# Seven-product stage: key rope, query norm and query rope one gate pair later, bank copies first; first products of the last projection ahead of the last head

## The chip, the cores and the metric

One core of a Trainium2 chip runs the program. Its engines work side by side, each through its own queue in order: TensorE (PE) multiplies matrices into the eight banks of PSUM, VectorE (DVE) and ScalarE (ACT) work element by element, GpSimd (POOL) and SyncE (SP) issue transfers. The metric is the device time of one execution in microseconds, as the median of several runs.

## What is computed

A trunk of two layers over a sequence of 1024 positions with 1024 features, all in float32. The first layer is a gated linear recurrence. The second is attention with eight heads whose keys and values come from a compressed vector; a gate multiplies its result ahead of the output projection. The part that the change touches is this one:

```python
def mla_shared_kv(x_stream, norm_kv, w_dkv, kv_norm, w_uk, w_uv, cos, sin):
    h = rms_norm(x_stream, norm_kv)
    ckr = h @ w_dkv
    c_kv = rms_norm(ckr[..., :KV_RANK], kv_norm)
    k_rope = apply_rope(ckr[..., KV_RANK:], cos[None], sin[None])
    k_nope = jnp.einsum("bsc,chd->bshd", c_kv, w_uk)
    v = jnp.einsum("bsc,chd->bshd", c_kv, w_uv)
    return k_nope, k_rope, v

def mla_layer(x, norm_g, w_in, q_norm, w_uq, w_out, k_nope, k_rope, v, cos, sin):
    h = rms_norm(x, norm_g)
    u = h @ w_in
    c_q = rms_norm(u[..., :Q_RANK], q_norm)
    gate = u[..., Q_RANK:]
    q = jnp.einsum("bsc,chd->bshd", c_q, w_uq)
    q_nope = q[..., :QK_NOPE]
    q_rope = apply_rope(q[..., QK_NOPE:], cos[None, :, None], sin[None, :, None])
    o = causal_block_attention(q_nope, q_rope, k_nope, k_rope, v)
    y = o.reshape(bsz, seq, N_HEADS * V_DIM) * jax.nn.silu(gate)
    return y @ w_out
```

A last norm over the features closes the trunk.

## The kernel before

Every float32 operand of a product is split into a high and a low part, and three matmuls (L114, L115, L116: high by high, low by high, high by low) stand for one. ACT rounds the high part (L82), DVE subtracts it for the low part (L83). A tile is 128 partitions by 512 elements; `hs(h)` is one of the two halves of the sequence, `page()` a tile of 128 by 1024 from a ring of 36, `tk()` a half tile from a ring of 8.

The linear recurrence fills the first 360 us or so. Then comes the stage that the names call `pair(m, ...)`. It makes two output blocks of 128 features for both halves of the sequence, four blocks of products, with seven products in place of eight, in the manner of Strassen. A product (`fmul`) is 12 matmuls, a pair 84. PE makes them into four PSUM banks a, c, b, d in the order a, c, b, a again, d, c again, d again. Between them banks are copied by ACT (`copy`, L611): a into b, once a's first product is there, then c into a spare tile `cc`, b into d, and b into a spare tile `v2`; the next product is added onto the copy. DVE takes the results out (L631, L162). The weights of a product are tiles `wa`, scaled by ACT (L507), summed by DVE (L519) and split (`wh`, `wl`).

Six such pairs follow one another, with other work between them: pair 0 gives the compressed key and value (`kvt`), pair 2 the key's rope input `krt` and the first third of the query, pair 4 the other two thirds (`qt`). Then come four gate pairs, `pair(6 + j)` with j = 0, 2, 4 and 6, numbered 6, 8, 10 and 12, each giving the gates of two heads, which ACT passes through Silu (L786) and POOL's queue stores in `gd`. The last of them takes its banks (`pm`) from the attention's pool, on the same PSUM. Work of the query and key lies beside the gate pairs:
- the key rope (L748 to L751): per half three DVE operations and a `spill`, which splits the result and stores it;
- the query's norm: its sums of squares on PE in the middle of pair 6 (L685), DVE's root (L150, L151), then multiplications of `qt` (L698, the function `multiplies` in `normed`) and a split of the six halves into `cq`;
- the query rope, `qrope(g)`: 72 matmuls in eight banks, and for each of four bank pairs two sums of two multiplications on DVE (L764 to L766), each split by ACT and DVE and stored by POOL's queue.

Program order gives the order of the work, with one correction: instructions are placed by a scheduler, in whose eyes those inside `tc.high_priority(offset=n)` stand n earlier. The order on each engine is then fixed; an engine waits for the instruction at the head of its queue. The copies have offset 120 (`WPC`) in before.

The attention runs over 64 items, a head and a block of 128 queries: scores (L867 to L871), a softmax (reduce L874, exponent L877, normalising L879), transposes (L887) and, for four blocks together, the product with the values, `pv` (L902 to L904), whose result DVE multiplies by the gate (L906) and splits. `pv` runs `PVD` items after its blocks, three after in head 6's second half. The last projection runs after the last head, but 36 of its matmuls (`dpart`, 12 parts of three) are placed inside the last head by the table `D_AT`. `wout` loads a block of its weight and makes the low part (L933); `yload` brings back the results of earlier heads.

Of the kernel before, what the change touches and what calls it, by code (L numbers as in the profile page):

```python
# [12 lines left out]
ALU = mybir.AluOpType  # L13
# [8 lines left out]
NH = 8  # L22
# [4 lines left out]
NPAGES = 36  # L27
NSPILL = 6
WPRI = 100
WOUT_AT = (-1, 1, 2)  # L30
YL_AT = (0, 0, 0, 0, 1, 2)
DSTART = 0
DPART = tuple((dt, k, k + 1) for dt in range(2) for k in range(6))
DEPQ = "gpsimd"
LOOK = 2
KQ_AT = (1, 0, 1, 0, 2, 0, 0, 0)
V0_AT = (1, 1, 2, 0)
V_AT = (0, 0, 0, 0, 0, 0, 1, 1)
D_AT = (0, 4, 1, 1, 1, 0, 3, 2)
PVD = 1  # L40
VQB = 4
HW = 512
# [7 lines left out]
GADD = ()  # L50
NWA = 7
WPC = 120


NA, CW, CB, BR, BI, LAM, NKV, KVN, NB, QN, FN, NVEC = 0, 8, 48, 58, 68, 78, 88, 96, 98, 106, 109, 117
# [2 lines left out]
def trunk(tc, xT, wina, vecs, wgate, wouta, winc, wuk, wuv, wuq, wuqr, woutb, rope, outT):  # L58
# [64 lines left out]
    def hs(h):  # L123
        return slice(h * HW, (h + 1) * HW)
# [478 lines left out]
    def pair(m, dst, w, banks, raw=(False, False), mid=None):  # L603

        a, c, b, d = banks
        cc = tcp.tile([P, HW], F32, tag="cc", bufs=2, name=nm("cc"))
        v2 = tcp.tile([P, HW], F32, tag="v2", name=nm("v2"))

        def copy(dst_, src, scale=1.0):
            with tc.high_priority(offset=WPC):  # L610
                A.activation(out=dst_, in_=src, func=AF.Copy, scale=scale)  # L611

        fmul(a, w[0], 0, True)
        copy(b, a, -1.0)
        fmul(c, w[1], 1, True)
        copy(cc, c)
        fmul(b, w[2], 2, False)
        fmul(a, w[3], 4, False)
        copy(d, b)
        copy(v2, b)  # L620
        fmul(d, w[4], 3, False)
        rest = mid() if mid else None

        def put(i, h, src):
            if raw[i]:
                A.activation(out=dst[i][h], in_=src, func=AF.Copy)
            else:
                byr(dst[i][h], src, r1[:, hs(h)])

        def put2(i, h, x, y):  # L630
            V.tensor_tensor(out=dst[i][h], in0=x, in1=y, op=ALU.subtract)  # L631
            if not raw[i]:
                byr(dst[i][h], dst[i][h], r1[:, hs(h)])

        put2(1, 1, d, cc)
        put(0, 0, a)
        fmul(c, w[5], 6, False)
        put2(0, 1, c, v2)
        fmul(d, w[6], 5, False)
        put(1, 0, d)  # L640
        if rest:
            rest()

    def wa():
        return tcp.tile([P, HW], F32, tag="wa", bufs=NWA, name=nm("wa"))
# [1 line left out]
    def four():  # L647
        return [pst() for _ in range(4)]

    def halves(t):  # L650
        return [t[:, hs(0)], t[:, hs(1)]]
# [36 lines left out]
    def normed(ts, acc, ps_, gcol, fac):  # L688
        n = len(ts)
        gs = con.tile([P, n], F32, name=nm("gs"))  # L690
        V.tensor_scalar(out=gs, in0=vec[:, gcol:gcol + n], scalar1=-0.5 * fac, scalar2=None, op0=ALU.mult)
        total(acc, ps_, P * n)

        def multiplies():
            for h in range(2):
                for j in range(n):
                    t = ts[j][:, hs(h)]
                    V.scalar_tensor_tensor(out=t, in0=t, scalar=gs[:, j:j + 1], in1=acc[h], op0=ALU.mult, op1=ALU.mult)  # L698

        return multiplies  # L700
# [8 lines left out]
    kvps = presum(kvacc)  # L709
    krt = page(F32)  # L710
    qt = [page(F32) for _ in range(3)]
    pair(2, [halves(krt), halves(qt[0])], wpair(2, wa), four(), (False, True), lambda: normed(kvt, kvacc, kvps, KVN, 1.0))
    square(qt, qacc, 0)


# [27 lines left out]
    for j in range(1, 3):  # L743
        square(qt, qacc, j)
    qps = presum(qacc)
    for h in range(2):
        x, y = krt[:, hs(h)], krs[:, hs(h)]
        V.tensor_tensor(out=x, in0=x, in1=cs[:, hs(h)], op=ALU.mult)  # L748
        V.scalar_tensor_tensor(out=y, in0=y, scalar=sgn, in1=sn[:, hs(h)], op0=ALU.mult, op1=ALU.mult)
        V.tensor_tensor(out=x, in0=x, in1=y, op=ALU.add)  # L750
        spill(4, h, x)  # L751


    qsd = dp.tile([4, 2 * P, S], F32, name="qsd")
# [18 lines left out]
    for j in range(0, NH, 2):  # L773
        gts = [[tk(), tk()] for _ in range(2)]
        w = wpair(6 + j, wa)
        if j < NH - 2:
            banks = four()
        else:

            pp.close()  # L780
            pss = es.enter_context(tc.tile_pool(name="pss", bufs=2, space=PSUM, reuse_waits="tile"))
            banks = [pss.tile([P, HW], F32, tag="pm", bufs=4, name=nm("pm")) for _ in range(4)]
        pair(6 + j, gts, w, banks, mid=None if j else lambda: normed(qt, qacc, qps, QN, SCALE))
        for i in range(2):
            for h in range(2):
                A.activation(out=gts[i][h], in_=gts[i][h], func=AF.Silu)  # L786
                DQ.dma_start(out=gd[j + i, :, hs(h)], in_=gts[i][h])
        if j == 0:
            cq = []
            for t in qt:  # L790
                cq.append((page(), page()))
                for h in range(2):
                    hl(t[:, hs(h)], cq[-1][0][:, hs(h)], cq[-1][1][:, hs(h)])
            cs, sn = tables()
        elif j == 2:
            for g in range(2):
                qrope(g)

# [159 lines left out]
    for i, (hd, qb) in enumerate(items):  # L958
# [19 lines left out]
        g = qb // 4  # L978
        if qb % 4 == 0:
            pts[hd, g] = [tuple(tp.tile([P, 4, HW], F32R, tag=f"pt{i}", name=nm("pt")) for i in range(2)) for _ in range(g + 1)]  # L980

        if late and i - late[0][0] >= (PVD if (hd, qb) < (NH - 2, 4) or hd == NH - 1 else 3):
            pv(*late.pop(0)[1:])
        transposes(qb, pend.pop((hd, qb)), pts[hd, g])
        if qb % 4 == 3:
# [138 lines left out]
```

## Time and profile before

| what | us |
|---|---|
| median of 3 runs (873.95 to 874.32) | 874.07 |
| the profiled execution's own time | 874.96 |
| its span | 873.2 |
| PE busy | 856.7 |
| DVE busy | 659.2 |
| ACT busy | 517.1 |
| POOL busy | 73.6 |

The mean granted clock of PE is 0.995 of full speed. A row of the timeline reads: start, duration, engine, line, operation, output and inputs with their shapes, how many, and in brackets the idle time of the engine ahead of it and what ended it. A row of waits reads: who waited for whom, total in us, how often, the longest. A matmul of 512 columns is shown as 0.39 us long, but they overlap: one starts each 0.227 us. In the same way DVE's and ACT's rows overlap by some 0.1 us.

### The profile page before, as it was taken

What the parts mean: (1) busy time and instruction counts of PE and PEld (TensorE: products, weight loads), DVE (VectorE), ACT (ScalarE), POOL (GpSimd) and SP (SyncE); (2) the same over time, 40 slices, a digit from 0 to 9 for tenths busy, and PEclk for the clock granted to TensorE, in tenths of its full rate; (3) what the DMA queues carried; (4) which work ended last, traced back from release to release, by engine and by line L of the source; (5) the groups of instructions that cost most, each with busy time, mean ns of one, the idle gap of its engine ahead of it and who ended that gap; (6) DMA issues with size and microseconds to landing.
All of it is one profiled execution on the core that took longest, in us unless ns stands there. A gap on an engine that the chain in (4) does not pass through costs nothing.

```text
span 873.2 us, 12181 instructions
## 1 busy us (share of the span) xinstructions
PE 856.7 (98%) x4326; PEld 729.3 (84%) x4326; DVE 659.2 (75%) x1222; ACT 517.1 (59%) x956; POOL 73.6 (8%) x143
## 2 busy tenths in 40 slices
PE   8999999999999999999999999999999999999995
PEld 7788888888888888888778889888998998888995
DVE  6898788777877764769889957888797887775453
ACT  7457787777687543699885545555565554431222
POOL 1010110011000100001211320000000000010000
PEclk9999999999999999999999999999999999999998
DMA  8333333333213544133545674122231326666032
GB/s 292 96 97 97 97 96 98 109 101 93 79 37 91 169 156 152 49 108 114 184 143 176 215 242 132 52 88 91 70 112 67 116 63 259 217 210 207 27 125 67
DMA packets 51789, 109.00 MB, mean 125 GB/s; under 512 B 6544, under 2 KB 16656, under 8 KB 51728
## 3 DMA queue, kind: packets, MB, share of 16 engines
q1 hardware_dynamic: 35968, 67.19, 24.0%
q0 software_dynamic: 15216, 40.51, 14.1%
q8 instruction: 34, 0.56, 0.3%
q10 hardware_dynamic: 544, 0.52, 0.2%
q14 instruction: 27, 0.22, 0.1%
HBM read 81.46 MB, written 26.21 MB: 123 GB/s over the span
## 4 chain that ended last, share of the span: by engine, by line
PE 90%; ACT 3%; DVE 3%; DMA 1%; issue 1%; POOL 0%; DVEq 0%; SPq 0%; ACTq 0%; POOLq 0%
PE ps L114 17%; PE ps L115 17%; PE ps L116 17%; PE pm L116 6%; PE pm L115 6%; PE pm L114 6%; PE pm L887 3%; PE pm L903 2%; PE pm L904 2%; PE s L868 2%; PE pm L902 2%; PE s L870 2%; PE s L869 2%; PE s L871 2%; PE s L867 2%
## 5 line engine op out<-in xcount | busy, mean ns | idle before, releaser
L114 PE MATMUL ps<-pg,wh 128*128 128x512 f32 x672 | 263.1, 392 | 4.7 <-ACT ps L611 2.2
L115 PE MATMUL ps<-pg,wh 128*128 128x512 f32 x672 | 262.1, 390 | 0.0
L116 PE MATMUL ps<-pg,wl 128*128 128x512 f32 x672 | 262.1, 390 | 0.1
L114 PEld LDWEIGHTS ps<-pg,wh 128*128 128x128 f32 x672 | 126.5, 188 | 33.7 <-ACT ps L611 3.9
L116 PEld LDWEIGHTS ps<-pg,wl 128*128 128x128 f32 x672 | 126.4, 188 | 26.8 <-DVE wl L83 0.4
L115 PEld LDWEIGHTS ps<-pg,wh 128*128 128x128 f32 x672 | 126.5, 188 | 26.6 <-DVE pg L262 0.5
L82 ACT ACTIVATE pt<-pm 128x512 fp32r<-128x512 f32 (+2 forms) x96 | 44.3, 490 | 59.3 <-PE pm L887 54.5
L877 ACT ACTIVATE pg<-s,m 128x128 f32<-128x128 f32 (+3 forms) x64 | 47.5, 743 | 45.1 <-DVE m L874 40.3
L114 PE MATMUL pm<-pg,pg 128*128 128x256 f32 (+1 forms) x192 | 61.9, 322 | 0.0
L115 PE MATMUL pm<-pg,pg 128*128 128x256 f32 (+1 forms) x192 | 61.6, 321 | 0.0
L116 PE MATMUL pm<-pg,pg 128*128 128x256 f32 (+1 forms) x192 | 61.3, 319 | 0.0
L83 DVE TENSOR_TENSOR pt<-pm,pt 128x512 fp32r<-128x512 f32 (+2 forms) x96 | 50.5, 547 | 2.3 <-ACT pt L82 2.3
L874 DVE TENSOR_REDUCE m<-s 128x1 f32<-128x128 f32 (+3 forms) x64 | 48.1, 754 | 1.1
L82 ACT ACTIVATE wh<-wr 128x512 fp32r<-128x512 f32 (+2 forms) x57 | 30.9, 543 | 25.9 <-PE ps L115 15.2
L358 DVE SCALAR_TENSOR_TENSOR t<-xb,vec,t 128x512 f32<-128x512 f32 x60 | 44.8, 747 | 0.4
L83 DVE TENSOR_TENSOR wl<-wr,wh 128x512 fp32r<-128x512 f32 (+2 forms) x57 | 32.9, 579 | 16.0 <-ACT wh L82 15.8
L82 ACT ACTIVATE pg<-pg 128x512 fp32r<-128x512 f32 x42 | 26.1, 630 | 30.1 <-DVE pg L412 17.9
L887 PE MATMUL pm<-ident,pg 128*128 128x128 f32 x288 | 42.3, 274 | 0.7 <-DVE pg L906 0.7
L116 PE MATMUL pm<-pg,wl 128*128 128x512 f32 x108 | 42.3, 392 | 0.0
L115 PE MATMUL pm<-pg,wh 128*128 128x512 f32 x108 | 42.3, 392 | 0.0
L114 PE MATMUL pm<-pg,wh 128*128 128x512 f32 x108 | 42.1, 390 | 0.0
L114 PEld LDWEIGHTS pm<-pg,pg 128*128 128x128 f32 x192 | 36.6, 191 | 2.6 <-issue 0.2
(226 smaller groups left out, 1787.5 us busy)
## 6 DMA issues: line engine op xcount, KB each, us to landing
wr<-wina SPq DMA_DIRECT2D x40, 256.0 KB, 2.9
wh<-wina POOLq DMA_DIRECT2D x36, 256.0 KB, 2.9
wa<-winc SPq DMA_DIRECT2D x24, 256.0 KB, 3.1
ysd<-pg POOLq DMA_DIRECT2D x12, 512.0 KB, 3.2
pg<-ysd SPq DMA_DIRECT2D x12, 512.0 KB, 9.9
wr<-wouta SPq DMA_DIRECT2D x16, 256.0 KB, 2.7
t<-xT SPq DMA_DIRECT2D x16, 256.0 KB, 3.8
x1d<-t POOLq DMA_DIRECT2D x16, 256.0 KB, 2.5
```

What stands on the lines that cost most here:

```text
L82: A.activation(out=hi, in_=src, func=AF.Copy)
L83: V.tensor_tensor(out=lo, in0=src, in1=f(hi), op=ALU.subtract)
L114: T.matmul(out=ps, lhsT=w[0], rhs=r[0], start=first, stop=False, skip_group_check=more)
L115: T.matmul(out=ps, lhsT=w[0], rhs=r[1], start=False, stop=False, skip_group_check=more)
L116: T.matmul(out=ps, lhsT=w[1], rhs=r[0], start=False, stop=last, skip_group_check=more)
L358: V.scalar_tensor_tensor(out=xc, in0=xb[:, j:j + HW], scalar=cwv[j], in1=xc, op0=ALU.mult, op1=ALU.add)
L867: T.matmul(out=sc[:, c], lhsT=q[0][:, ql], rhs=k[0][:, c], start=True, stop=False)
L868: T.matmul(out=sc[:, c], lhsT=q[0][:, ql], rhs=k[1][:, c], start=False, stop=False)
L869: T.matmul(out=sc[:, c], lhsT=q[1][:, ql], rhs=k[0][:, c], start=False, stop=False)
L874: V.tensor_reduce(out=m, in_=sc, axis=AX.X, op=ALU.max, negate=True)
L877: A.activation(out=p_[:, 0:nk], in_=sc, func=AF.Exp, bias=m, accum_out=l)
L887: T.transpose(out=ps[:, (b - b0) * P:(b - b0 + 1) * P], in_=p_[:, b * P:(b + 1) * P], identity=ident)
```

## The change

- The copies' offset becomes 600 (`WPB`); that of the other work that uses `WPC` stays at 120.
- The key rope becomes a function and is issued after pair 6 in place of before it.
- `pair` hands back the function of the norm's multiplications in place of calling it. For the query it is called after pair 8 (before: at the end of pair 6), and the split into `cq` goes with it. For the compressed key and value it is called at once, as before.
- `qrope` is issued after pair 10 (before: after pair 8).
- In the last head, the first weight block of the last projection is loaded and split four items earlier, `yload` begins five items earlier, and the parts of three matmuls are spread by another table from one item earlier on.
- `pv` of head 6's second half runs one item after its blocks, in place of three.

```diff
--- before.py
+++ after.py
@@ -27,16 +27,16 @@
 NPAGES = 36
 NSPILL = 6
 WPRI = 100
-WOUT_AT = (-1, 1, 2)
-YL_AT = (0, 0, 0, 0, 1, 2)
-DSTART = 0
+WOUT_AT = (-5, 1, 2)
+YL_AT = (-5, -4, 0, 0, 1, 2)
+DSTART = -1
 DPART = tuple((dt, k, k + 1) for dt in range(2) for k in range(6))
 DEPQ = "gpsimd"
 LOOK = 2
 KQ_AT = (1, 0, 1, 0, 2, 0, 0, 0)
 V0_AT = (1, 1, 2, 0)
 V_AT = (0, 0, 0, 0, 0, 0, 1, 1)
-D_AT = (0, 4, 1, 1, 1, 0, 3, 2)
+D_AT = (2, 0, 3, 1, 1, 1, 0, 2, 2)
 PVD = 1
 VQB = 4
 HW = 512
@@ -50,6 +50,7 @@
 GADD = ()
 NWA = 7
 WPC = 120
+WPB = 600
 
 
 NA, CW, CB, BR, BI, LAM, NKV, KVN, NB, QN, FN, NVEC = 0, 8, 48, 58, 68, 78, 88, 96, 98, 106, 109, 117
@@ -607,7 +608,7 @@
         v2 = tcp.tile([P, HW], F32, tag="v2", name=nm("v2"))
 
         def copy(dst_, src, scale=1.0):
-            with tc.high_priority(offset=WPC):
+            with tc.high_priority(offset=WPB):
                 A.activation(out=dst_, in_=src, func=AF.Copy, scale=scale)
 
         fmul(a, w[0], 0, True)
@@ -638,8 +639,7 @@
         put2(0, 1, c, v2)
         fmul(d, w[6], 5, False)
         put(1, 0, d)
-        if rest:
-            rest()
+        return rest
 
     def wa():
         return tcp.tile([P, HW], F32, tag="wa", bufs=NWA, name=nm("wa"))
@@ -709,7 +709,7 @@
     kvps = presum(kvacc)
     krt = page(F32)
     qt = [page(F32) for _ in range(3)]
-    pair(2, [halves(krt), halves(qt[0])], wpair(2, wa), four(), (False, True), lambda: normed(kvt, kvacc, kvps, KVN, 1.0))
+    pair(2, [halves(krt), halves(qt[0])], wpair(2, wa), four(), (False, True), lambda: normed(kvt, kvacc, kvps, KVN, 1.0))()
     square(qt, qacc, 0)
 
 
@@ -743,12 +743,14 @@
     for j in range(1, 3):
         square(qt, qacc, j)
     qps = presum(qacc)
-    for h in range(2):
-        x, y = krt[:, hs(h)], krs[:, hs(h)]
-        V.tensor_tensor(out=x, in0=x, in1=cs[:, hs(h)], op=ALU.mult)
-        V.scalar_tensor_tensor(out=y, in0=y, scalar=sgn, in1=sn[:, hs(h)], op0=ALU.mult, op1=ALU.mult)
-        V.tensor_tensor(out=x, in0=x, in1=y, op=ALU.add)
-        spill(4, h, x)
+
+    def krope():
+        for h in range(2):
+            x, y = krt[:, hs(h)], krs[:, hs(h)]
+            V.tensor_tensor(out=x, in0=x, in1=cs[:, hs(h)], op=ALU.mult)
+            V.scalar_tensor_tensor(out=y, in0=y, scalar=sgn, in1=sn[:, hs(h)], op0=ALU.mult, op1=ALU.mult)
+            V.tensor_tensor(out=x, in0=x, in1=y, op=ALU.add)
+            spill(4, h, x)
 
 
     qsd = dp.tile([4, 2 * P, S], F32, name="qsd")
@@ -780,19 +782,23 @@
             pp.close()
             pss = es.enter_context(tc.tile_pool(name="pss", bufs=2, space=PSUM, reuse_waits="tile"))
             banks = [pss.tile([P, HW], F32, tag="pm", bufs=4, name=nm("pm")) for _ in range(4)]
-        pair(6 + j, gts, w, banks, mid=None if j else lambda: normed(qt, qacc, qps, QN, SCALE))
+        rest = pair(6 + j, gts, w, banks, mid=None if j else lambda: normed(qt, qacc, qps, QN, SCALE))
         for i in range(2):
             for h in range(2):
                 A.activation(out=gts[i][h], in_=gts[i][h], func=AF.Silu)
                 DQ.dma_start(out=gd[j + i, :, hs(h)], in_=gts[i][h])
         if j == 0:
+            krope()
+            qnorm = rest
+        elif j == 2:
+            qnorm()
             cq = []
             for t in qt:
                 cq.append((page(), page()))
                 for h in range(2):
                     hl(t[:, hs(h)], cq[-1][0][:, hs(h)], cq[-1][1][:, hs(h)])
             cs, sn = tables()
-        elif j == 2:
+        elif j == 4:
             for g in range(2):
                 qrope(g)
 
@@ -978,8 +984,7 @@
         g = qb // 4
         if qb % 4 == 0:
             pts[hd, g] = [tuple(tp.tile([P, 4, HW], F32R, tag=f"pt{i}", name=nm("pt")) for i in range(2)) for _ in range(g + 1)]
-
-        if late and i - late[0][0] >= (PVD if (hd, qb) < (NH - 2, 4) or hd == NH - 1 else 3):
+        if late and i - late[0][0] >= PVD:
             pv(*late.pop(0)[1:])
         transposes(qb, pend.pop((hd, qb)), pts[hd, g])
         if qb % 4 == 3:
```

In these rows of an engine's order stand line, operation, output, inputs and size; the numbers in the names tell tiles apart and differ between the kernels. First ACT, around the end of the query rope. Before, the pair behind the rope is pair 10: `tk` rows of L82 are splits of the rope, `wh` rows splits of weights, L611 the copy of bank a into b.

```order
L82 ACTIVATE tk_825_4267<-tk_824_4266 128x512
L82 ACTIVATE wh_862_4438<-ws_861_4436 128x512
L82 ACTIVATE tk_827_4276<-tk_826_4275 128x512
L82 ACTIVATE tk_831_4305<-tk_830_4304 128x512
L82 ACTIVATE wh_864_4443<-ws_861_4436 128x512
L507 ACTIVATE wa_895_4616<-wa_895_4616,vec_66 128x128 x4
L82 ACTIVATE tk_833_4314<-tk_832_4313 128x512
L82 ACTIVATE wh_867_4453<-wa_866_4447 128x512
L82 ACTIVATE wh_869_4458<-wa_856_4414 128x512
L611 ACTIVATE ps_877_4473<-ps_875_4471 128x512
L82 ACTIVATE tk_843_4355<-tk_842_4354 128x512
```

Now the pair behind the rope is pair 12, whose banks are named `pm`:

```order
L83 ACTIVATE wh_891_4607<-ws_890_4605 128x512
L83 ACTIVATE tk_856_4445<-tk_855_4444 128x512
L83 ACTIVATE tk_860_4474<-tk_859_4473 128x512
L83 ACTIVATE wh_893_4612<-ws_890_4605 128x512
L83 ACTIVATE tk_862_4483<-tk_861_4482 128x512
L83 ACTIVATE wh_896_4622<-wa_895_4616 128x512
L83 ACTIVATE tk_872_4524<-tk_871_4523 128x512
L83 ACTIVATE tk_874_4533<-tk_873_4532 128x512
L83 ACTIVATE tk_878_4562<-tk_877_4561 128x512
L83 ACTIVATE tk_880_4571<-tk_879_4570 128x512
L83 ACTIVATE wh_898_4627<-wa_885_4583 128x512
L612 ACTIVATE pm_906_4646<-pm_904_4644 128x512
```

Four splits of the rope stood ahead of the copy before, with a fifth behind it; now all eight do (the first is the row ahead of those shown), and the weight split `wh_898`.

On DVE, the end of the rope's work in the changed kernel (L766 and L767 are the multiplications, L768 the sums, the L84 rows with `tk` the low parts of the splits):

```order
L766 TENSOR_TENSOR tk_873_4532<-ps_869_4503,pg_815_4231 128x512
L767 TENSOR_TENSOR tk_874_4533<-ps_870_4504,pg_814_4230 128x512
L84 TENSOR_TENSOR tk_871_4523<-tk_871_4523,tk_872_4524 128x512
L768 TENSOR_TENSOR tk_873_4532<-tk_873_4532,tk_874_4533 128x512
L766 TENSOR_TENSOR tk_877_4561<-ps_875_4541,pg_814_4230 128x512
L767 TENSOR_TENSOR tk_878_4562<-ps_876_4542,pg_815_4231 128x512
L84 TENSOR_TENSOR tk_873_4532<-tk_873_4532,tk_874_4533 128x512
L768 TENSOR_TENSOR tk_877_4561<-tk_877_4561,tk_878_4562 128x512
L766 TENSOR_TENSOR tk_879_4570<-ps_875_4541,pg_815_4231 128x512
L767 TENSOR_TENSOR tk_880_4571<-ps_876_4542,pg_814_4230 128x512
L84 TENSOR_TENSOR tk_877_4561<-tk_877_4561,tk_878_4562 128x512
L768 TENSOR_TENSOR tk_879_4570<-tk_879_4570,tk_880_4571 128x512
```

Between the fourth sum and the eighth, which is the last row here, stand these rows and six more; of pair 12's weights only one split and one sum lie among them.

Second, ACT in the first gate pair, from the copy of a into b to the two copies of bank b. Before:

```order
L611 ACTIVATE ps_768_3911<-ps_766_3909 128x512
L82 ACTIVATE tk_737_3822<-tk_635_3280 128x512
L507 ACTIVATE wa_801_4102<-wa_801_4102,vec_66 128x128
L82 ACTIVATE tk_739_3826<-tk_636_3281 128x512
L82 ACTIVATE tk_741_3833<-pg_663_3430 128x512
L611 ACTIVATE cc_770_3913<-ps_767_3910 128x512
L82 ACTIVATE wh_762_3901<-wa_757_3885 128x512
L507 ACTIVATE wa_856_4414<-wa_856_4414,vec_66 128x128 x4
L82 ACTIVATE wh_764_3905<-wa_749_3864 128x512
L611 ACTIVATE ps_769_3912<-ps_768_3911 128x512
L611 ACTIVATE v2_771_3914<-ps_768_3911 128x512
```

And now:

```order
L612 ACTIVATE ps_766_3895<-ps_764_3893 128x512
L83 ACTIVATE tk_737_3822<-tk_635_3280 128x512
L508 ACTIVATE wa_793_4074<-wa_793_4074,vec_66 128x128
L83 ACTIVATE tk_739_3826<-tk_636_3281 128x512
L83 ACTIVATE wh_760_3885<-wa_755_3869 128x512
L612 ACTIVATE cc_768_3897<-ps_765_3894 128x512
L508 ACTIVATE wa_820_4238<-wa_820_4238,vec_66 128x128 x4
L83 ACTIVATE wh_762_3889<-wa_747_3848 128x512
L612 ACTIVATE ps_767_3896<-ps_766_3895 128x512
L612 ACTIVATE v2_769_3898<-ps_766_3895 128x512
```

The split of the key rope (`tk_741`) has left; the four scalings (L507) and the weight split stay ahead of the copies of bank b.

Third, DVE where head 6 ends. A block's normalising (L879) has the width of its keys, 896 for the block before the last, 1024 for the last; head 7's first block has 128. Before, from two rows behind the normalising of the block before the last:

```order
L83 TENSOR_TENSOR pg_1422_7088<-pm_1456_7268,pg_1421_7087 128x512
L83 TENSOR_TENSOR pt_1458_7278<-pm_1461_7281,pt_1457_7277 128x4x128
L872 TENSOR_TENSOR s_1463_7292<-s_1463_7292,mask_80 128x128
L874 TENSOR_REDUCE m_1464_7304<-s_1463_7292 128x1
L83 TENSOR_TENSOR pt_1458_7278<-pm_1467_7311,pt_1457_7277 128x4x128
L872 TENSOR_TENSOR s_1469_7323<-s_1469_7323,mask_80 128x128
L874 TENSOR_REDUCE m_1470_7330<-s_1469_7323 128x1
L878 RECIPROCAL l_1466_7307<-l_1466_7307 128x1
L879 TENSOR_SCALAR pg_1465_7306<-pg_1465_7306,l_1466_7307 128x1024
L878 RECIPROCAL l_1472_7333<-l_1472_7333 128x1
L879 TENSOR_SCALAR pg_1471_7332<-pg_1471_7332,l_1472_7333 128x128
L906 TENSOR_TENSOR pg_1414_7073<-pm_1473_7337,pg_1414_7073 128x512
```

And now, from the normalising (L885) of the third last block, 768 wide, on:

```order
L885 TENSOR_SCALAR pg_1448_7228<-pg_1448_7228,l_1449_7229 128x768
L880 TENSOR_REDUCE m_1458_7265<-s_1457_7253 128x1
L939 TENSOR_TENSOR pg_1454_7245<-wr_1455_7246,pg_1453_7244 128x512
L939 TENSOR_TENSOR pg_1454_7245<-wr_1456_7250,pg_1453_7244 128x512
L884 RECIPROCAL l_1460_7268<-l_1460_7268 128x1
L912 TENSOR_TENSOR pg_1414_7073<-pm_1467_7294,pg_1414_7073 128x512
L885 TENSOR_SCALAR pg_1459_7267<-pg_1459_7267,l_1460_7268 128x896
L84 TENSOR_TENSOR pg_1422_7088<-pm_1461_7272,pg_1421_7087 128x512
L84 TENSOR_TENSOR pg_1422_7088<-pm_1462_7281,pg_1421_7087 128x512
L84 TENSOR_TENSOR pg_1469_7309<-pg_1414_7073,pg_1468_7308 128x512
L84 TENSOR_TENSOR pt_1464_7291<-pm_1470_7312,pt_1463_7290 128x4x128
```

The two subtractions of the first weight block (L939) and the gate product of head 6's first half (L912, before L906) now stand ahead of the normalising of the block before the last, and so ahead of the last block's.

## The prediction

> **What bounds the kernel now.** The page comes first: its engine table, its chain, and the row of the costliest group.
>
> ```profile
> span 873.2 us, 12181 instructions
> ...
> PE 856.7 (98%) x4326; PEld 729.3 (84%) x4326; DVE 659.2 (75%) x1222; ACT 517.1 (59%) x956; POOL 73.6 (8%) x143
> ...
> PE 90%; ACT 3%; DVE 3%; DMA 1%; issue 1%; POOL 0%; DVEq 0%; SPq 0%; ACTq 0%; POOLq 0%
> ...
> L114 PE MATMUL ps<-pg,wh 128*128 128x512 f32 x672 | 263.1, 392 | 4.7 <-ACT ps L611 2.2
> ```
>
> TensorE (PE) is busy for 98% of the span and makes up 90% of the chain. The diff neither adds nor removes a matmul, so only PE's idle time can change, and the clock at which PE runs. Next come the waits of PE between 20 and 860 us, and, of the timeline, the matmul behind each of the larger ones:
>
> ```profile
> PE ps L114 <- ACT ps L611: 2.2, 3, 1.3
> PE ps L114 <- DVE tk L631: 1.1, 1, 1.1
> PE pm L887 <- DVE pg L906: 0.7, 1, 0.7
> PE pm L903 <- DVE pt L83: 0.3, 1, 0.3
> ```
>
> ```profile
> 430.75 0.50 PE L114 MATMUL ps<-pg,wh 128*128 128x512 f32 x1 [1.31 <-ACT ps L611]
> ...
> 437.09 0.50 PE L114 MATMUL ps<-pg,wh 128*128 128x512 f32 x1 [0.60 <-ACT ps L611]
> ...
> 447.67 0.50 PE L114 MATMUL ps<-pg,wh 128*128 128x512 f32 x1 [1.15 <-DVE tk L631]
> ```
>
> That is all there is to win: 1.31 + 0.60 + 1.15 = 3.1 us in the first gate pair, 0.3 in the pair before it, and 0.7 + 0.3 = 1.0 in the last head. A pause longer than about 4 us does not exist inside the kernel, so a new one would count in full.
>
> **Bank copies and the first gate pair: 0.** The higher priority should let the copies (L611) pass other work on ACT. For each of the three waits I ask what ends last, by ACT's and DVE's timelines:
>
> ```profile
> 421.98 0.60 ACT L626 ACTIVATE pg<-ps 128x512 f32<-128x512 f32 x1 [2.01 <-DMA kvd<-pg]
> ...
> 430.12 0.58 ACT L611 ACTIVATE ps<-ps 128x512 f32<-128x512 f32 x1
> ...
> 434.75 1.28 ACT L507 ACTIVATE wa<-wa,vec 128x128 f32<-128x128 f32 x4 [0.23 <-DMA wa<-winc]
> 435.94 0.61 ACT L82 ACTIVATE wh<-wa 128x512 fp32r<-128x512 f32 x1
> 436.46 0.57 ACT L611 ACTIVATE ps<-ps 128x512 f32<-128x512 f32 x1
> ```
>
> ```profile
> 441.99 0.69 DVE L83 TENSOR_TENSOR wl<-ws,wh 128x512 fp32r<-128x512 f32 x1 [1.29 <-ACT wh L82]
> ...
> 446.93 0.68 DVE L631 TENSOR_TENSOR tk<-ps,cc 128x512 f32<-128x512 f32 x1
> ```
>
> The first wait goes back to a spill that ACT waits for at 421.98; behind that, the changed order has the same ACT rows up to the copy at 430.12. The second copy still stands behind four scalings of a weight tile (L507), which start when its DMA lands, at 434.75. What leaves the queue ahead of it is a split of the key rope, which had room in front of that DMA. The third is DVE's queue of ten operations between 441.99 and 447.5; they are all still there. So I take no gain here. The ends are 0 and -3.4 (all four waits gone). The 0.3 of the pair before may go, but the matmul at 430.75 then waits that much longer, since its copy is tied to the spill.
>
> **Query rope behind the third gate pair: +7.2.** This is the large term. ACT works its queue in order: the copy of bank a into bank b, for which PE waits two products into a pair, cannot start before the rows ahead of it. Before, four of the query rope's eight splits stood ahead of it in the pair behind the rope; now, by the order shown with the change, all eight do, and PE's rope is followed at once by the last gate pair. How late the splits are is read from before, where the rope also runs:
>
> ```profile
> 466.86 0.39 PE L114 MATMUL ps<-pg,wh 128*128 128x512 f32 x1
> ...
> 483.18 0.39 PE L114 MATMUL ps<-pg,wh 128*128 128x512 f32 x1
> ```
>
> ```profile
> 482.45 0.68 DVE L766 TENSOR_TENSOR tk<-tk,tk 128x512 f32<-128x512 f32 x1
> ...
> 496.13 0.69 DVE L766 TENSOR_TENSOR tk<-tk,tk 128x512 f32<-128x512 f32 x1
> ```
>
> ```profile
> 483.21 0.63 ACT L82 ACTIVATE tk<-tk 128x512 fp32r<-128x512 f32 x1 [0.18 <-ACT wa L507]
> 483.75 0.62 ACT L82 ACTIVATE wh<-wa 128x512 fp32r<-128x512 f32 x1
> ...
> 486.47 0.58 ACT L611 ACTIVATE ps<-ps 128x512 f32<-128x512 f32 x1
> ```
>
> Let T be the rope's first matmul, 466.86 in before. The rope has 72 matmuls and ends at 483.18, T + 16.3, so one takes 0.227 us. The next pair's two first products are 24 matmuls, 5.4 us. PE is therefore due at the third product at T + 21.8. In before the copy ran at 486.47, T + 19.6, and was in time by 2 us; the matmul follows a copy by 430.75 - 430.12 = 0.63.
>
> Now the changed kernel. DVE makes eight sums (L766), each behind two multiplications, and each sum releases one split on ACT. The fourth sum stood at 482.45, T + 15.6, in before; the work up to it is the same in both. From there to the eighth, DVE's changed queue has 18 instructions: 8 multiplications, 4 sums, 4 low-part subtractions, one weight split and one weight sum. DVE had no pause there in before: 22 steps from 482.45 to 496.13 make 0.62 each, so 18 take 11.2. The eighth sum starts at T + 26.8 and ends at T + 27.5. Behind it on ACT stand the eighth split, one weight split and the copy. A split occupies the queue for 0.54 (483.21 to 483.75), so the copy starts at T + 28.6 and PE at T + 29.2. That is 7.4 late, or 7.0 if a step is 0.60. I take 7.2. Ends: 5.4 if DVE needs 0.5 for a step, 8.5 if the last weight split's DMA or bank adds a microsecond. The wait is not hidden: the last pair's two first products are all that PE has, and behind the copy wait the remaining 60 matmuls and the attention. That the third pair now has no rope ahead of it frees nothing, since in before its copy was in time.
>
> **The clock behind that pause: +1.7.** No pause of this length is in the trace, so I bound the price. The nearest rows are those of the start, a matmul behind a pause and the windows that follow (their columns are length, busy time of PE, PEld, DVE, ACT and POOL, granted clock, DMA share), and, on the other side, the first gate pair's window:
>
> ```profile
> 6.11 0.51 PE L114 MATMUL ps<-pg,wh 128*128 128x512 f32 x1 [1.38 <-ACT wh L82]
> ```
>
> ```profile
> 7.00:9.00 2.00, 2.00 (x4) 1.11 (x5) 1.23 (x2) 0.97 (x2) 0.00 (x0) 0.60 1.02 396
> 9.00:10.80 1.80, 1.80 (x5) 1.43 (x5) 0.70 (x2) 1.67 (x2) 0.00 (x0) 0.50 0.96 373
> ...
> 430.00:449.00 19.00, 16.50 (x70) 12.97 (x71) 15.61 (x26) 14.80 (x35) 2.22 (x4) 1.00 0.37 122
> ```
>
> In the start the clock stood at half for about 2 x 0.8 + 1.8 = 3.4 us; work at half clock loses half of that, 1.7. Pauses of 1.3 us in mid-kernel cost no clock. A pause of 7 us is nearer to the sparse start than to these, so I take one such stretch, 1.7, with ends at 0 and 3.4 (two stretches).
>
> [...]
>
> **Key rope and query norm one pair later: 0.** They are the same DVE and ACT instructions, now beside the gate pairs 8 and 10 in place of 6 and 8. DVE's share there is the cover:
>
> ```profile
> 449.00:468.00 19.00, 19.00 (x86) 15.71 (x85) 16.83 (x28) 17.59 (x39) 3.79 (x7) 1.00 0.66 209
> 483.00:503.00 20.00, 20.00 (x90) 16.58 (x89) 19.65 (x33) 10.86 (x20) 7.58 (x14) 1.00 0.63 219
> ```
>
> The pair at 449 to 468 leaves DVE 2.2 us and ACT 1.4 us of room. The normalising of the query, 6 products and 12 splits, moves out of it, and the key rope's 6 products and its splits and four spills come in. The rope's own window leaves DVE 0.35 us; its work is what leaves. The spills go through the POOL queue, which is busy for 3.79 of 19 us. If the room were missed in either pair, the price is a copy late by one or two ACT rows, at most 1 us together.
>
> **First products of the last projection ahead of the last head: +0.4.** The waits there, and the rows they come from:
>
> ```profile
> 740.42 0.45 PE L902 MATMUL pm<-pt,pg 128*128 128x512 f32 x1
> ...
> 742.34 0.62 PE L887 MATMUL pm<-ident,pg 128*128 128x128 f32 x4
> ...
> 744.30 1.42 PE L887 MATMUL pm<-ident,pg 128*128 128x128 f32 x11 [0.74 <-DVE pg L906]
> ...
> 747.28 0.50 PE L903 MATMUL pm<-pt,pg 128*128 128x512 f32 x1 [0.33 <-DVE pt L83]
> ```
>
> ```profile
> 743.56 0.68 DVE L906 TENSOR_TENSOR pg<-pm,pg 128x512 f32<-128x512 f32 x1
> ...
> 750.73 1.28 DVE L933 TENSOR_TENSOR pg<-wr,pg 128x512 fp32r<-128x512 f32 x2
> ```
>
> These waits hang on the softmax chain of head 6's last query block. The p times v product of that head's first half (12 matmuls, 740.42 to 742.34, 1.9 us) now runs ahead of that block's scores, its gate product (L906, 0.6 from start to start) and the first weight's two subtractions (1.2) stand ahead of its normalising on DVE. The chain is later by 1.9 + 0.6 + 1.2 = 3.7. PE has 1.9 of that as moved work and 6 of the 36 pulled-forward matmuls of the last projection, 1.4, as cover: 3.3. So 0.4 more of waiting; ends -1.0 (both waits covered) and +1.3 (the subtractions in full).
>
> **Sum.** Against the profiled execution's own time, 874.96 with a span of 873.2, the change is +7.2 + 1.7 + 0.4 = +9.3. The median of the runs shown is 874.07, 0.9 lower, and the timed runs are what is forecast: 874.07 + 9.3 = **883.4**.
>
> **The rivals.**
> (a) The wait comes but the clock holds: 874.07 + 7.2 + 0.4 = 881.7. For it speaks that no mid-kernel pause lowered the clock, against it that none was over 1.5 us. 0.22.
> (b) The wait comes, and the first gate pair's copies do pass: 883.4 - 3.4 = 880.0. Against it stand the DMA at 434.75 and the spill at 421.98, which no priority moves. 0.08.
> (c) Two stretches at half clock in place of one, since the pause drops the clock late or the clock rises late: 883.4 + 1.7 = 885.1. For it: the pause is five times as long as the one at 6.11. Against it: the start, which had one stretch. [...] 0.12.
> (d) The other side: DVE keeps pace with PE's rope, the last pair's copy is in time, and the four early waits and the last head's go: 874.07 - 3.4 - 1.0 = 869.7. It decides at the copy's start: T + 21.1 or sooner, which needs the eighth sum by T + 19.3. For it: some of the 18 steps are weight work that could come sooner. Against it: before's DVE had its fourth sum only at T + 15.6. 0.05.
> (e) The change does not do what it says: ACT's order comes out such that the copy passes the splits, and the copies elsewhere stay where they were. Then nothing but the last head moves: 874.5. Against it is the order. 0.04.
>
> **How the numbers follow.** The forecast, 883.4, has 0.49. Cases below it reach to 880.0 with (a) and (b); the term's own ends (5.4, and a last head at -1.0) take these to about 878. Above, (c) gives 885.1 and a rope wait of 8.5 with it 886.4. The range from 878.3 to 886.5 leaves out (d), (e) and some of each edge, about 0.15. A measurement of this kernel can tell about 0.2%, 1.7 us, from no change: faster is (d), 0.05, with 0.01 of (e); same is the rest of (e) and 0.01 of the low edge, 0.04; slower is 0.90.
>
> **What would show it.** Right: one matmul in the last gate pair with some 7 us of waiting for the copy's line, the granted clock at half behind it, the waits of 1.31, 0.60 and 1.15 in the first gate pair much as before, and no further wait over 1 us in pairs 8 and 10. Wrong: the copy in the last pair starting sooner than T + 25, the waits of the first gate pair gone, a clock of 1.00 right behind the pause, or more than 2 us lost or won between 735 and 752 us of before.

## The result, and the profile after

The changed kernel takes 885.06 us (median of 6 runs, 884.13 to 886.21) against 874.29 for the one before (6 runs, two of them at 877.4). The ratio is 1.0117, with a 95% interval of 1.0106 to 1.0128: slower by some 10 us. The median is inside the predicted range and 1.7 above the predicted 883.4. The page of the profiled execution (886.21, the slowest of the six, with a mean granted clock of 0.989 where the others have 0.991 to 0.993) begins so; the third row is the chain:

```profile
span 884.4 us, 12168 instructions
...
PE 861.1 (97%) x4326; PEld 731.5 (83%) x4326; DVE 659.1 (75%) x1222; ACT 517.0 (58%) x956; POOL 73.3 (8%) x143
...
PE 87%; DVE 4%; ACT 4%; DMA 3%; issue 1%; POOL 0%; SPq 0%; DVEq 0%; ACTq 0%; POOLq 0%
```

DVE's and ACT's work is the same to 0.1 us. PE does the same matmuls, yet is busy for 4.4 us longer, which means that some of them ran slower. The waits of PE between 20 and 870 us:

```profile
PE pm L115 <- ACT pm L612: 7.0, 1, 7.0
PE ps L115 <- ACT ps L612: 1.4, 3, 0.9
PE ps L115 <- DVE tk L632: 1.1, 1, 1.1
PE pm L908 <- DVE pt L84: 1.1, 1, 1.1
PE pm L116 <- DMA pg<-ysd: 0.8, 1, 0.8
PE pm L117 <- DVE pg L939: 0.4, 1, 0.4
PE s L873 <- ACT pg L883: 0.3, 1, 0.3
```

One wait of 7.0 us on a bank copy is new (L612 was L611), and four small ones in the last head. The timeline of PE shows where the first three rows lie:

```profile
430.82 0.50 PE L115 MATMUL ps<-pg,wh 128*128 128x512 f32 x1 [0.93 <-ACT ps L612]
...
436.84 0.50 PE L115 MATMUL ps<-pg,wh 128*128 128x512 f32 x1 [0.27 <-ACT ps L612]
...
447.35 0.50 PE L115 MATMUL ps<-pg,wh 128*128 128x512 f32 x1 [1.12 <-DVE tk L632]
...
485.58 0.39 PE L115 MATMUL ps<-pg,wh 128*128 128x512 f32 x1
...
514.54 0.79 PE L115 MATMUL pm<-pg,wh 128*128 128x512 f32 x1 [7.04 <-ACT pm L612]
```

The first gate pair's waits are all still there, 0.93 + 0.27 + 1.12 where 1.31 + 0.60 + 1.15 stood. The rope begins at 485.58 (T), and PE stands still ahead of the last pair's third product. DVE's last sum and ACT's rows ahead of the copy:

```profile
512.13 0.69 DVE L768 TENSOR_TENSOR tk<-tk,tk 128x512 f32<-128x512 f32 x1
```

```profile
512.85 0.63 ACT L83 ACTIVATE tk<-tk 128x512 fp32r<-128x512 f32 x1 [1.77 <-DVE tk L768]
513.39 0.61 ACT L83 ACTIVATE wh<-wa 128x512 fp32r<-128x512 f32 x1
513.91 0.58 ACT L612 ACTIVATE pm<-pm 128x512 f32<-128x512 f32 x1
```

The eighth split waits for the eighth sum; behind it come the weight split and the copy, one upon another. The windows behind the pause, with the granted clock as the third number from the right:

```profile
514.40:516.00 1.60, 1.46 (x4) 1.18 (x5) 1.09 (x2) 1.11 (x3) 1.50 (x3) 0.50 0.92 320
516.00:518.00 2.00, 2.00 (x6) 1.61 (x5) 0.00 (x0) 0.00 (x0) 1.65 (x4) 0.50 1.12 369
518.00:520.00 2.00, 2.00 (x6) 1.52 (x6) 0.00 (x0) 0.31 (x1) 0.00 (x0) 0.50 0.95 338
...
521.00:522.00 1.00, 1.00 (x6) 0.81 (x5) 0.05 (x1) 0.32 (x1) 0.00 (x0) 1.00 0.98 369
```

From 514.54 to 520.25 thirteen matmuls follow one another at 0.43 us, the first at 0.59, where 0.227 is the rule: 2.8 us lost. At last the waits of the last head, on PE and, for the largest, on DVE:

```profile
754.99 0.49 PE L116 MATMUL pm<-pg,pg 128*128 128x512 f32 x1 [0.80 <-DMA pg<-ysd]
...
773.18 0.50 PE L117 MATMUL pm<-pg,pg 128*128 128x512 f32 x1 [0.39 <-DVE pg L939]
...
789.41 0.50 PE L908 MATMUL pm<-pt,pg 128*128 128x512 f32 x1 [1.09 <-DVE pt L84]
```

```profile
787.46 1.28 DVE L939 TENSOR_TENSOR pg<-wr,pg 128x512 fp32r<-128x512 f32 x2
788.66 1.28 DVE L84 TENSOR_TENSOR pt<-pm,pt 128x512 fp32r<-128x512 f32 x2
```

At 754.99 a pulled-forward matmul itself waits for the reload of an earlier head's result. At 789.41 the last product with the values waits for the last split of p, which on DVE stands behind two weight subtractions. These two stood ahead of that split before, too (775.66 and 776.86); what differs is PE's own work at this place, first before, then now:

```profile
775.47 1.04 PE L887 MATMUL pm<-ident,pg 128*128 128x128 f32 x8
776.26 0.48 PE L115 MATMUL pm<-pg,pg 128*128 128x512 f32 x1
...
777.27 0.39 PE L116 MATMUL pm<-pg,pg 128*128 128x512 f32 x1
777.60 0.50 PE L902 MATMUL pm<-pt,pg 128*128 128x512 f32 x1
```

```profile
787.28 1.03 PE L893 MATMUL pm<-ident,pg 128*128 128x128 f32 x8
789.41 0.50 PE L908 MATMUL pm<-pt,pg 128*128 128x512 f32 x1 [1.09 <-DVE pt L84]
```

From the last transposes to the product it is 2.13 us in both kernels. Before, five matmuls of the parts ran in this time; now nothing does.

Adding up along PE: at the attention's first scores the changed kernel is 9.75 us behind (537.81 against 528.06), at the last norm's sum 11.78 (875.29 against 863.51). So the stage cost 9.75 = 7.2 of pause from start to start, 2.8 of slow clock, and -0.3; the last head cost 2.0.

### The profile page after: what moved, and what is told of

It reads as the page before. It is cut to its first block, busy times and chain, and to the rows that moved or that the text cites. A ratio compares the mean times of both kernels' runs of the same rounds, so it can differ in the third digit from the quotient of the medians.

```text
span 884.4 us, 12168 instructions
## 1 busy us (share of the span) xinstructions
PE 861.1 (97%) x4326; PEld 731.5 (83%) x4326; DVE 659.1 (75%) x1222; ACT 517.0 (58%) x956; POOL 73.3 (8%) x143
## 4 chain that ended last, share of the span: by engine, by line
PE 87%; DVE 4%; ACT 4%; DMA 3%; issue 1%; POOL 0%; SPq 0%; DVEq 0%; ACTq 0%; POOLq 0%
PE ps L116 16%; PE ps L115 16%; PE ps L117 16%; PE pm L117 6%; PE pm L116 6%; PE pm L115 6%; PE pm L893 3%; PE pm L910 2%; PE pm L909 2%; PE s L873 2%; PE s L874 2%; PE s L876 2%; PE s L875 2%; PE s L877 2%; PE pm L908 2%
## 5 line engine op out<-in xcount | busy, mean ns | idle before, releaser
L116 PEld LDWEIGHTS ps<-pg,wh 128*128 128x128 f32 x672 | 126.4, 188 | 26.8 <-DVE pg L263 0.6
L84 DVE TENSOR_TENSOR pt<-pm,pt 128x512 fp32r<-128x512 f32 (+2 forms) x96 | 50.6, 548 | 1.2 <-ACT pt L83 1.0
L115 PE MATMUL pm<-pg,wh 128*128 128x512 f32 x108 | 43.5, 403 | 7.0 <-ACT pm L612 7.0
L84 DVE TENSOR_TENSOR wl<-wr,wh 128x512 fp32r<-128x512 f32 (+2 forms) x57 | 32.9, 579 | 17.0 <-ACT wh L83 16.1
L116 PE MATMUL pm<-pg,wh 128*128 128x512 f32 x108 | 43.4, 401 | 0.0
```

The lines of the kernel that those rows point to most:

```text
L84: V.tensor_tensor(out=lo, in0=src, in1=f(hi), op=ALU.subtract)
L115: T.matmul(out=ps, lhsT=w[0], rhs=r[0], start=first, stop=False, skip_group_check=more)
L116: T.matmul(out=ps, lhsT=w[0], rhs=r[1], start=False, stop=False, skip_group_check=more)
```

## The experiments

All ratios are to the kernel before, run on the same chip in the same job; the median of before lay between 874.5 and 874.9.

**1. The rope's position alone.** The kernel before, with one line changed:

```diff
-        elif j == 2:
+        elif j == 4:
             for g in range(2):
                 qrope(g)
```

> The kernel before with the query rope alone moved behind the third gate pair; norm, key rope, priorities and last head as before. Queue theory (the copy of bank a stands on ACT behind all eight splits of the rope, and DVE makes their sums at 0.6 us a step): one wait of about 7.0 us at the third product of the last gate pair, about 2.6 us lost at half clock behind it, the early waits of 1.3, 0.6 and 1.15 as before, the last head as before: 874.1 + 7.0 + 2.6 = 883.7 us, between 882.5 and 885. Rival (the wait needs the norm and its split moved along with it, as more work on DVE and ACT beside the rope): a wait under 4 us, no half clock, under 879 us.

884.37 us (4 runs), ratio 1.0107 (1.0092 to 1.0122). The waits of PE begin with:

```profile
PE pm L114 <- ACT pm L611: 7.0, 1, 7.0
PE ps L114 <- ACT ps L611: 1.6, 3, 0.9
PE ps L114 <- DVE tk L631: 1.4, 1, 1.4
```

The wait is 7.0 us without any of the other edits; nine matmuls at half clock behind it lose 2.0. The rival falls: the norm and key rope need not have moved for it.

**2. The last head back.** The changed kernel with the four tables and the delay of before:

```diff
-WOUT_AT = (-5, 1, 2)
-YL_AT = (-5, -4, 0, 0, 1, 2)
-DSTART = -1
-D_AT = (2, 0, 3, 1, 1, 1, 0, 2, 2)
+WOUT_AT = (-1, 1, 2)
+YL_AT = (0, 0, 0, 0, 1, 2)
+DSTART = 0
+D_AT = (0, 4, 1, 1, 1, 0, 3, 2)
-        if late and i - late[0][0] >= PVD:
+        if late and i - late[0][0] >= (PVD if (hd, qb) < (NH - 2, 4) or hd == NH - 1 else 3):
```

> The changed kernel with the last head as before (tables of weight loads, reloads and parts, the start of the parts, three items of delay for head 6's second half). If the last head's new waits (for the reload's DMA, for DVE's weight subtraction, and at the last product with the values) cost 2 us net, 885.0 - 2.0 = 883.0 us, and between head 6 and the end the gaps of before. Rival (what looks like 2 us is the profiled run's longer stretch at half clock): 885 us, no change.

883.01 us (4 runs), ratio 1.0097 (1.0077 to 1.0117). As expected to the tenth, though runs of this kernel scatter by 3 us; the pause of 7.0 and 13 slow matmuls are unchanged, and the last head has the waits of before again, 0.7 and 0.3. The interval of the ratio reaches up to the changed kernel's 1.0117, so the time alone does not settle it; the sixth experiment does.

**3. Filling the pause.** The changed kernel with the last pair's second product made three times:

```diff
-        fmul(c, w[1], 1, True)
+        for _ in range(3 if m == 12 else 1):
+            fmul(c, w[1], 1, True)
```

> The changed kernel with the second product of the last gate pair made three times in place of once: 24 matmuls, 5.4 us of work for PE inside the pause of 7 us; the last of the three is the one that counts. If the clock falls because PE stands still for 7 us: the wait falls to about 1.6 us, the granted clock stays at 1.00 behind it, and the time falls by the 2.6 us lost at half clock, to 882.4 us. Rival (the clock falls at this place for another reason, or with a pause of 1.6 us as well): 13 matmuls at half clock behind the wait as now, 885 us.

883.28 us (4 runs, 882.18 to 885.13), ratio 1.0097 (1.0081 to 1.0113). The time alone would be weak evidence; the rows are not. The matmul behind the pause, and the window that begins with it:

```profile
513.73 0.50 PE L115 MATMUL pm<-pg,wh 128*128 128x512 f32 x1 [1.60 <-ACT pm L612]
```

```profile
513.70:516.00 2.30, 2.27 (x10) 1.88 (x11) 0.99 (x2) 1.01 (x2) 2.30 (x5) 1.00 0.59 135
```

PE has 5.4 us more to do, goes on with the third product 29.0 us after the rope's first matmul, as in the changed kernel, and the clock stays at 1.00. So the slow stretch comes from PE's standing still, not from the place in the program. Three of the four runs have a mean granted clock of 0.997; the fourth, 885.13, has 0.993, and where it lost its clock is not known.

**4. Half the rope.** The kernel before, its second rope half behind the third gate pair:

```diff
-        elif j == 2:
-            for g in range(2):
-                qrope(g)
+        elif j in (2, 4):
+            qrope(j // 2 - 1)
```

> The kernel before with the query rope in two halves: the first behind the second gate pair, as before, the second behind the third; all else as before. Four splits then stand ahead of the last pair's copy. Queue theory: PE is due at the third product 60 matmuls (13.6 us) after the half rope's first; DVE's fourth sum starts 16 rows of 0.6 us behind the multiplication that waits for the second bank, at 4.45 + 9.6 = 14.1 us, ends at 14.7, then a split, a weight split and the copy, 0.55, 0.55 and 0.63: 16.4 us. A wait of 2.8 us in the last pair and none in the third; no half clock, since the pause is shorter than the windows that fell: 874.1 + 2.9 = 877.0 us. Rival 1 (only the whole rope overloads DVE; half of it is absorbed): no wait, 874 us. Rival 2 (any pause over 2 us drops the clock): 2.9 + 2.0 to 2.7, 879 to 879.7 us.

879.11 us (4 runs), ratio 1.0047 (1.0032 to 1.0062). The wait is 2.95, where 2.8 was worked out row by row; the third pair has none. My word on the clock was wrong for the profiled execution (880.43):

```profile
511.44 0.50 PE L114 MATMUL pm<-pg,wh 128*128 128x512 f32 x1 [2.95 <-ACT pm L611]
```

```profile
511.40:513.00 1.60, 1.56 (x6) 1.29 (x7) 1.00 (x2) 1.01 (x2) 1.60 (x4) 0.86 0.99 389
513.00:515.00 2.00, 2.00 (x7) 1.51 (x6) 0.00 (x0) 0.00 (x0) 0.77 (x2) 0.50 1.11 297
```

The clock holds for 1.0 to 1.5 us behind the pause and then falls to half: 1.6 us lost. The queue theory holds in its second dose. For the clock, rival 2 holds in this execution, the slowest of the four, with a mean granted clock of 0.992. The other three have 0.995 to 0.997. All executions traced here with such a stretch have 0.989 to 0.993, all without one 0.995 to 0.997, so the pause of 2.95 seems to have dropped the clock in one execution of four.

**5. Without the splits.** The changed kernel, rope's second half stored unsplit:

```diff
                 V.tensor_tensor(out=t1, in0=t1, in1=t2, op=op)
+                if g:
+                    DQ.dma_start(out=qsd[c, g * P:(g + 1) * P, hs(h)], in_=t1)
+                    DQ.dma_start(out=qsd[2 + c, g * P:(g + 1) * P, hs(h)], in_=t1)
+                    continue
                 th, tl = parts(t1, t2.bitcast(F32R))
```

> The changed kernel without the four splits of the rope's second half: its sums are stored unsplit, as high and as low part alike, so the low parts are left out there. On ACT four rows fewer stand ahead of the last pair's copy, on DVE three rows fewer of 0.6 us stand among the 18 ahead of the eighth sum. If ACT's queue position holds PE: the copy needs only its bank, which DVE's multiplication of the fifth sum pair frees at about 20.5 us after the rope's first matmul, and PE is due at 21.8: a wait of 0 to 0.5 us, no half clock, 885.2 - 7.2 - 2.6 = 875.4 us. Rival (DVE's pace or the banks hold PE, wherever the splits stand): three rows fewer, 7.0 - 1.9 = 5.1 us of wait and half clock still: 883 us.

883.04 us (4 runs), ratio 1.0091 (1.0071 to 1.0110). By its time the rival wins, by its trace it loses. ACT's copy, and then a row of ACT and one of PE at the attention's start:

```profile
506.02 0.58 ACT L612 ACTIVATE pm<-pm 128x512 f32<-128x512 f32 x1 [1.03 <-DVE tk L766]
...
524.35 0.63 ACT L83 ACTIVATE wh<-wr 128x512 fp32r<-128x512 f32 x1 [5.92 <-DMA wr<-wuv]
```

```profile
531.44 0.33 PE L877 MATMUL s<-pg,pg 128*128 128x128 f32 x1 [3.42 <-ACT pg L83]
```

The copy runs at 506.02 with four splits ahead of it in place of eight, released by the multiplication (L766) that frees its bank, and the last pair has no wait at all. DVE's eighth sum begins 3.1 us after PE has gone on with the third product, at 507.05:

```profile
510.15 0.69 DVE L768 TENSOR_TENSOR tk<-tk,tk 128x512 f32<-128x512 f32 x1
```

DVE's backlog alone does not hold PE; the place behind the last splits on ACT does. No run left DVE's rows as they are and put only the copy ahead of the splits. But 3.4 us of waiting come back at the first scores, with a further slow stretch behind: the granted clock is 0.50 from 532.0 to 538.3. The transfer of `wuv` takes 10.4 us there against 3.3 in the changed kernel, by the DMA issues between 500 and 540 us, first of this run, then of the changed kernel:

```profile
wr<-wuv SPq DMA_DIRECT2D x3, 256.0 KB, 10.4
```

```profile
wr<-wuv SPq DMA_DIRECT2D x3, 256.0 KB, 3.3
```

In the same 40 us the rope's stores take 3.9 us each (median) against 2.6, and the reloads of the key's pages 10.8 against 7.3. What makes all of these slow was not shown: no run moved the transfers apart. Whether the pause of the changed kernel covers such a wait there, too, or whether this run alone has it, stays open.

**6. The last head alone.** The kernel before with the second experiment's lines the other way round.

> The kernel before with the last head's part of the change alone. By the changed kernel's trace (net 2.0 us more of gaps between head 6's end and the last product with the values): 874.5 + 2.0 = 876.5 us, with waits for the reload's DMA, for DVE's weight subtraction and for DVE's split at the last product with the values. Rival (the prediction's term): +0.4, 874.9 us; or the part costs only behind the long pause, where the timing is shifted: 874.5 us.

877.13 us (10 runs), ratio 1.0022 (1.0013 to 1.0031): 1.9 us by the ratio, 2.4 by the medians. It shows the same gaps as the changed kernel: the reload's 0.80, the subtraction's 0.39, and 1.09 at the last product. The prediction's +0.4 was wrong, and the long pause has no part in it.

**7. Parts issued late.** The changed kernel with fewer parts inside the head:

```diff
-D_AT = (2, 0, 3, 1, 1, 1, 0, 2, 2)
+D_AT = (0, 0, 3, 1, 1, 1, 0, 2, 0)
...
-    while late:
-        pv(*late.pop(0)[1:])
     while dwork:
         dwork.pop(0)()
+    while late:
+        pv(*late.pop(0)[1:])
```

> The changed kernel with four of the twelve parts taken from item 55 and from the last item and issued behind all transposes, ahead of the last product with the values; PE's order has five of their matmuls between the last transposes and that product, as before. If the parts pulled ahead cost by waiting for the reload, and their absence at the end uncovers the last split: the gaps of 1.0 and 0.5 us at the first parts go, the gap of 1.7 us at the last product falls to about 0.5: 885.2 - 2.3 = 882.9 us. Rival (the waits only move, since the weights' subtractions set them): 885 us.

886.59 us (4 runs), ratio 1.0129 (1.0110 to 1.0148). The gaps at the last product and at the first parts are gone, as foreseen, but a new one stands where the parts were:

```profile
753.75 0.58 PE L873 MATMUL s<-pg,pg 128*128 128x256 f32 x1 [2.30 <-ACT pg L883]
```

So the parts at head 6's end do cover the softmax there; taking them away gives the wait back. The fix did not work: the ratio is not below the changed kernel's 1.0117.

**8. Copies first and key rope later, alone.** The kernel before with these two edits:

```diff
-            with tc.high_priority(offset=WPC):
+            with tc.high_priority(offset=600):
                 A.activation(out=dst_, in_=src, func=AF.Copy, scale=scale)
...
-    for h in range(2):
-        x, y = krt[:, hs(h)], krs[:, hs(h)]
-        ...
+    def krope():
+        for h in range(2):
+            x, y = krt[:, hs(h)], krs[:, hs(h)]
+            ...
...
         if j == 0:
+            krope()
```

> The kernel before with the copies' priority at 600 and the key rope behind the first gate pair; norm, rope and last head as before. By the changed kernel's trace the early waits fall by 0.3 us net (the gap of 0.4 in the pair before goes, the first gate pair's waits change by -0.4, -0.35 and 0, and one of the gains is given back at the spill): 874.2 us, 0 to 0.5 below before. Rival (the title's reading: with the copies first the three waits go): 3 us below before, 871.5 us.

874.45 us (12 runs), ratio 0.9994 (0.9985 to 1.0003). No difference that can be told. The three waits of the first gate pair are 0.81, 0.99 and 1.01.

**9 and 10. The last head's edits apart.** First only the delay of the product with the values (the last two lines of the second experiment's diff, the other way round), then only the four tables.

> The kernel before with one edit of the last head: the product with the values of head 6's second half runs one item behind its blocks instead of three. PE's order keeps five matmuls of the parts between the last transposes and the last product, so the last gap stays at about 0.1 us. The softmax chain of head 6's last block is later by the moved product and the gate product, 1.9 + 0.6 us, with 1.9 us of moved work as cover: +0.6, 875.1 us on this chip. Rival (this edit is the one that costs 2 us): 876.7 us.

> The kernel before with the other edits of the last head: weight loads, reloads and parts by the changed tables, the product with the values of head 6 as before. PE's order has no matmul of the parts between the last transposes and the last product. If the tables cost through the last split left uncovered (1.7 us in place of 0.1) and through DVE's subtraction (0.4 to 0.7): +2.0, less what the six parts cover in head 6 (up to 1): 875.7 to 876.7 us on this chip, with the gap of 1.7 us at the last product. Rival (the moved product with the values is what costs): 874.7 us and no such gap.

The delay alone: 875.22 (11 runs), ratio 1.0005 (0.9996 to 1.0014). The tables alone: 878.45 (5 runs), ratio 1.0037 (1.0025 to 1.0050). The tables carry the loss. Their trace has these two waits:

```profile
740.56 0.44 PE L887 MATMUL pm<-ident,pg 128*128 128x128 f32 x2 [1.21 <-DVE pg L83]
...
779.68 0.50 PE L902 MATMUL pm<-pt,pg 128*128 128x512 f32 x1 [1.09 <-DVE pt L83]
```

They take some 3 us by the ratio, more than both edits together. Two of the five runs, the profiled one among them, took 877.0, the other three 878.5 to 878.9, at mean granted clocks of 0.995 to 0.997 in all five; what the slower three lost besides is open.

**11. Filling half the pause.** As the third experiment, with the product made twice.

> The changed kernel with the second product of the last gate pair made twice: 12 matmuls, 2.7 us of work in the pause, which falls to about 4.3 us. If a pause of some 3 us is enough to drop the clock, and what it loses does not grow with the pause: 1.6 to 2.7 us at half clock as in the runs with 3.0 and 7.0, and the time stays at 885.2 us. Rival (the loss grows with the pause): 1.5 us or less lost, 884 us or less.

885.04 us (4 runs), ratio 1.0118 (1.0104 to 1.0132). The pause is 4.31:

```profile
513.30 0.80 PE L115 MATMUL pm<-pg,wh 128*128 128x512 f32 x1 [4.31 <-ACT pm L612]
```

Ten matmuls behind it are at half clock, 2.2 us lost. The loss has not shrunk with the pause.

**12. The harmless parts together.** Copies first, key rope later and the delay edit, on the kernel before.

> The two harmless parts of the change together on the kernel before: copies' priority 600, the key rope behind the first gate pair, and the product with the values of head 6's second half one item behind; norm, rope and tables as before. If the parts add up as their traces say (early gaps 0.6 less, last head 0.3 less): 874.7 - 0.9 = 873.8 us, ratio 0.999. Rival (each is within noise and the gains are given back at the next wait): 874.7 us, ratio 1.000.

874.31 us (11 runs), ratio 0.9994 (0.9985 to 1.0003). The parts do not add up to anything that can be measured, and no version beat the kernel before.

## Why the prediction came out right, point by point

**The rope's term held, by its own mechanism.** Worked out were a last sum at T + 26.8, a copy at T + 28.6 and PE at T + 29.2, 7.4 late, of which 7.2 was taken. With T at 485.58 the trace has 512.13, 513.91 and 514.54: T + 26.6, T + 28.3 and T + 29.0, 7.2 from start to start. The first experiment shows that the position alone makes the wait, the fourth that half the splits make 2.95, the fifth that ACT's queue is where it is made. The prediction did not ask what lies behind: in the fifth experiment, with the copy in time, the attention's start waits instead.

**The clock's term was sized too small.** The step was to take one stretch as in the start, 1.7, with 3.4 as its end. Measured were 2.8 in the profiled execution and the second experiment, 2.0 in the first, 1.8 in the seventh, all behind the same pause of 7.0. So 1.7 was the low edge of what comes, and the step failed in taking it as the middle. What sets the spread from 1.8 to 2.8 behind one and the same pause, no run shows; the step's ends, 0 and 3.4, hold all four.

**Copies, key rope and norm: right.** No gain was taken, since a spill, a weight's DMA and DVE's queue end last. In the changed kernel ACT still waits for the spill, until 421.91, and for the weight's DMA, until 434.50. The waits stayed at 2.3 of 3.1 us, and the eighth experiment is within noise. The other side, three waits gone, did not come. The norm's move has no run of its own; no wait of PE came up beside it.

**The last head was wrong: +0.4 against 2.0, past its end of +1.3.** The step that failed was to take the pulled-forward matmuls as cover and not to ask where they had come from. In before, five of them stood between the last transposes and the last product with the values, and covered the last split. The new table leaves none there, so PE stands still for 1.09 us ahead of 789.41. In before this place is at 777.60, outside the stretch of 735 to 752 us that the prediction looked at. One of the pulled ones waits for a reload's DMA besides, and a subtraction adds 0.4 of wait. The waits counted on to stay, 0.74 and 0.33, went. That the gap at the last product comes with the tables is shown by the ninth and tenth experiments; that issuing parts late closes it, by the seventh, which lost the gain elsewhere.

**The sum.** 7.2 + 1.7 + 0.4 = 9.3 was forecast; the trace has 7.2 + 2.8 - 0.3 + 2.0 = 11.7 up to the last norm's sum. Behind it the changed kernel's tail is 0.6 us shorter (884.4 - 875.29 against 873.2 - 863.51), so the spans differ by 11.2; the medians differ by 10.8. Two terms were too small in the same direction, and the range, wide for the clock, held. That the time came within 1.7 us is luck in part: 2.8 and 2.0 where 1.7 and 0.4 stood make 2.7 us, and the early waits and the shorter tail, which the prediction has at 0 or not at all, gave 0.9 back.

## What to carry to other kernels

When work moves along a queue, look at what short, urgent instruction will now stand behind it on each engine: a copy of half a microsecond held PE for seven, because eight splits were ahead of it, for which DVE had a sum ready only each 2.4 us. The copies' higher priority did not help here: with an offset of 120 (first experiment) and of 600 (the changed kernel) PE waits the same 7.0 us. Ask what each queue's head waits for. And work pulled forward to fill a hole leaves one where it stood.

## What the hardware showed

A pause of PE has a second price, which did not grow with the pause here. Behind pauses inside the kernel of 1.3 us (before), 1.6 (third experiment) and 1.8 (fourth, in the first gate pair, at 431.08) the clock stayed at 1.00. Behind 2.95, 3.42 (fifth), 4.31 and 7.04 it fell to 0.50. Lost were 1.6 us behind 2.95, 2.2 behind 4.31 and 1.8 to 2.8 behind 7.04; behind 3.42 an estimate from the 6.3 us at 0.50 is some 3. Only 7.04 was seen in more than one trace, in four. At 2.95 the fall came only 1.0 to 1.5 us after PE had started again and, by the mean granted clocks, in one execution of four.
